# Splitting weights by one copy and one subtraction of 1024 columns instead of two of 512

## The chip, the cores and the metric

The kernel runs on one core of one Trainium2 chip. The metric is the device time of one execution in microseconds (us). Three executions of the kernel before took 1092.47, 1092.65 and 1095.68 us; their median is 1092.65 us.

## What is computed

The reference is a trunk of two layers over 256 tokens of width 1024, all in float32:

```
for l in range(2):
    x = x + 0.5 * swiglu(rms_norm(x), w_gate, w_up, w_down)   # "f1", inner width 2816
    h = rms_norm(x)
    p = h @ w_in                                              # 1024 -> 3328 columns
    x = x + concat(rwkv7(p[:, :1792]), retnet(p[:, 1792:])) @ w_out
    x = x + 0.5 * swiglu(rms_norm(x), w_gate, w_up, w_down)   # "f2"
out = rms_norm(x)
```

The RWKV-7 part (8 heads of 64) is a recurrence with decays, computed by chunks of 64 tokens: products within a chunk, the inverse of a triangle, and a state handed from chunk to chunk. The retention part has 4 heads.

## The kernel before

**Precision.** A plain float32 product is not used for the large matrices. Each operand is split into a rounded part `hi` and the rest `lo`, both of type float32r, and a product is three matmuls into one accumulator: hi by hi (line 189), hi by lo (line 190), lo by hi (line 191), all in `mm3`. For the activations this split is made once per token tile; for the weights it is made on the fly, by ScalarE and VectorE.

**Weights.** All weights lie in DRAM as 2 x 83 pieces of 128 x 2048, and are used as halves of 128 x 1024 (512 KB), 332 halves in all. `half(i, h)` loads half `h` of piece `i` into one of three raw buffers (`NRAW = 3`, SyncE's queue, line 169), and then, for each of its two 512-column chunks, copies the chunk to `whi` on ScalarE (line 176) and subtracts on VectorE, `wlo = raw - whi` (line 177). A raw buffer is free for the next load when the last subtraction from it is done. The tiles `whi` and `wlo` are 512 columns wide, in rings; there are four kinds of rings, by the stage that uses the piece: kind 0 for both feed-forwards (pieces 0 to 32 and 50 to 82 of a layer), kind 1 for the first two pieces of the mixer's projections, kind 2 for the other eleven, kind 3 for the four of the output projection. `NHL = (5, 4, 5, 6)` gives the halves that each ring holds, so 10, 8, 10 and 12 tiles of 512.

**Order of the work.** Tokens are two tiles of 128, `t = 0` and `t = 1`. Each is a Python generator that walks through all stages and yields after about one half of weights; `run` takes turns between them, with `t = 1` two steps behind (`LAG = 2`). So a half of weights is loaded and split once, used by `t = 0` in 6 matmuls, and some steps later by `t = 1` in 6 more; only then are its tiles free. Between the mixer and the second feed-forward the distance is larger: tile 0 begins the feed-forward (line 278 and following) while tile 1 still has the end of its mixer before it (`PLAN`).

The program is written without semaphores. A planner in the compiler (`auto_bufs=True`) plays the program through with modelled times, fixes by them the order of each engine's instructions, gives each tile an address in SBUF by the time that it lives, and puts in the waits. So the order on an engine is fixed when the kernel is built; at run time each engine takes its instructions in that order, and an instruction that has to wait holds up those behind it on its engine.

**Other lines that matter here.** `norm_T` transposes x (line 253) and makes its two parts, `parts` (lines 257 and 258). Line 239 is ScalarE's Square over 1024 columns with a sum. Lines 290 and 291 are the gate of the feed-forward, `to_features` transposes its result (line 272) and splits it (lines 213 and 214). `layer_vecs` loads a layer's small vectors on ScalarE's queue and makes two small tables on VectorE (lines 159 and 160). In the mixer, lines 346 to 499 and 575 to 581 are VectorE's work between the projections; line 783 multiplies retention scores that line 778 has masked.

The descriptor scratch is not named in the kernel before, so it has the default size.

Of the kernel before, what the change touches and what calls it, by code (L numbers as in the profile page):

```python
# [10 lines left out]
F32 = mybir.dt.float32  # L11
F32R = mybir.dt.float32r
BF16 = mybir.dt.bfloat16
AF = mybir.ActivationFunctionType
ALU = mybir.AluOpType
# [5 lines left out]
P = 128  # L21
# [12 lines left out]
HOT = 5  # L34
DEFER = (0, 16, 0)
MV = (0, 0, 0, 0, 0, 1)
NHL = (5, 4, 5, 6)
FIRST = 2
LAG = 2
PLAN = ("mkrqegRvJabcW...w", "mkrqegRvJabcW.....w")  # L40
PAUSE = (0, 2)
# [27 lines left out]


class Tiles:
    """Tiles of SBUF under names of their own, of which any number may be alive."""

    def __init__(self, pool):
        self.pool, self.n = pool, 0
# [14 lines left out]
class Trunk:  # L90
# [50 lines left out]
            self.nc.sync.dma_start(self.x[t][:, w * n:w * n + w], self.x_d[t][:, w * n:w * n + w])  # L141

    def few(self, n, name, bufs=1):
        """A few columns of a tile that all small things share, reused in turn."""
        if name not in self.rings:
            self.rings[name] = [0, self.nsmall]
            self.nsmall += n * bufs
            assert self.nsmall <= NBASE
        ring = self.rings[name]
        c = ring[1] + n * (ring[0] % bufs)  # L150
        ring[0] += 1
        return self.c[:, c:c + n]
# [8 lines left out]
        self.layer = l  # L161

    def half(self, i, h):
        """Half a piece of weights, split into two parts of 12 bits each."""
        if (i, h) not in self.wq:
            nc = self.nc
            raw = self.raw[:, self.nraw % NRAW]
            self.nraw += 1
            nc.sync.dma_start(raw, self.w_d[i][:, 1024 * h:1024 * h + 1024])
            kind = sum(i % PIECES >= b for b in (33, 33 + FIRST, 46, 50)) % 4  # L170
            parts = []
            for c in range(2):
                hi = self.A.get([P, 512], f"whi{kind}", F32R, 2 * NHL[kind])
                lo = self.A.get([P, 512], f"wlo{kind}", F32R, 2 * NHL[kind])
                src = raw[:, 512 * c:512 * c + 512]
                nc.scalar.activation(hi, src, AF.Copy)  # L176
                nc.vector.tensor_tensor(lo, src, hi.bitcast(F32), op=ALU.subtract)  # L177
                parts.append((hi, lo))
            self.wq[i, h] = parts
        return self.wq[i, h]  # L180

# [11 lines left out]
            self.catch_up(t, 1)  # L193

    def defer(self, t, count, f):
        """Emits f after some more products of the projections, and its own behind those."""
        if count:
            self.later[t].append([count, f])
        else:
            f()  # L200

    def catch_up(self, t, n=99):
        """Emits what has been deferred long enough."""
        for d in self.later[t]:
            d[0] -= n
        while self.later[t] and self.later[t][0][0] <= 0:
            f = self.later[t].pop(0)[1]
            with self.tc.issue_after(self.recent.ins):
                f()
# [10 lines left out]
            self.nc.vector.tensor_copy(out, x)  # L220

    def rsqrt(self, y, nx):
        """y = (-2 nx)^-1/2: a guess from the exponent, and Newton's steps."""
        nc = self.nc
        I32 = mybir.dt.int32
        TT, STT = nc.vector.tensor_tensor, nc.vector.scalar_tensor_tensor
        w = self.few(y.shape[1], "newton", 2)
        nc.vector.tensor_scalar(y.bitcast(I32), nx.bitcast(I32), 1, 0x3fffffff, op0=ALU.logical_shift_right, op1=ALU.bitwise_xor)
        nc.vector.tensor_scalar(y, y, GUESS, None, op0=ALU.mult)
        for _ in range(3):  # L230
            TT(w, y, y, op=ALU.mult)
            TT(w, w, nx, op=ALU.mult)
            STT(y, w, 1.5, y, op0=ALU.add, op1=ALU.mult)
# [25 lines left out]
                                               op0=ALU.mult, op1=ALU.subtract)  # L259
        self.rms(t, col)  # L260

# [1 line left out]
    def ffn(self, t, col, base, pause=()):  # L263
        nc = self.nc
        self.norm_T(t, col)
# [47 lines left out]
                                           op0=ALU.mult, op1=ALU.add)  # L313
        yield

# [1 line left out]
    def proj_block(self, t, base, blk):  # L317
        h0 = 0 if blk == 0 else 1 + 2 * (blk - 1)
        width = 256 if blk == 0 else 512
# [33 lines left out]
        return bc(self.v[:, off:off + 4], [P, 4, n])  # L353

    def half_sigmoid(self, out, ps, col):
        """sigmoid(ps + bias) as 0.5 + 0.5 tanh of half the argument."""
        nc = self.nc
        for p in range(NPAIR):
            nc.scalar.activation(out[:, p, :], ps[:, p, :], AF.Tanh, scale=0.5, bias=self.hv[:, col + p:col + p + 1])
        nc.vector.tensor_scalar(out, out, 0.5, 0.5, op0=ALU.mult, op1=ALU.add)  # L360

    def rwkv_decay(self, t, ps):
        """Decay, learning rate and gate, and the products of the decays from the start of a chunk."""
        nc, A, z = self.nc, self.A, self.z[t]
        TT, ACT, STT = nc.vector.tensor_tensor, nc.scalar.activation, nc.vector.scalar_tensor_tensor
        full = [P, 4, P]
        e, o = slice(0, 64), slice(64, 128)
        m0 = self.shifted(t, ps, 2, 0, 0)
        ACT(m0[0:64, 0, :], m0[0:64, 0, :], AF.Tanh)
        ACT(m0[:, 1, :], m0[:, 1, :], AF.Tanh, scale=0.5)  # L370
        nc.vector.tensor_scalar(m0[:, 1, :], m0[:, 1, :], 0.5, 0.5, op0=ALU.mult, op1=ALU.add)
        zw = self.ppr.tile(full, F32, name="pre")
        za = self.ppr.tile(full, F32, name="pre")
        zg = self.ppr.tile(full, F32, name="pre")
        lw, lg = self.lora
        for p in range(NPAIR):
            nc.tensor.matmul(zw[:, p, :], lhsT=lw[0:64, p * P:(p + 1) * P], rhs=m0[0:64, 0, :], start=True, stop=True)
        for p in range(NPAIR):
            nc.tensor.matmul(za[:, p, :], lhsT=lw[64:128, p * P:(p + 1) * P], rhs=m0[64:128, 0, :], start=True, stop=True)
        for p in range(NPAIR):  # L380
            nc.tensor.matmul(zg[:, p, :], lhsT=lg[:, p * P:(p + 1) * P], rhs=m0[:, 1, :], start=True, stop=True)
        sw = A.get(full, "sw")
        self.half_sigmoid(sw, zw, 14)
        a = A.get(full, "a")
        self.half_sigmoid(a, za, 18)
        g = A.get(full, "g")
        ACT(g, zg, AF.Copy)
        cs = A.get([P, 512], "cs")
        nc.vector.tensor_tensor_scan(cs, self.scan, sw.rearrange("p a b -> p (a b)"), 0.0,
                                     op0=ALU.mult, op1=ALU.add)  # L390
        pr = A.get([P, 8, CH], "pr")
        csv = cs.rearrange("p (a b) -> p a b", a=8)
        ACT(pr, csv, AF.Exp, scale=-KAPPA)
        ip = A.get([P, 8, CH], "ip")
        ACT(ip, csv, AF.Exp, scale=KAPPA)
        pc = self.few(16, f"pc{t}")[0:64].rearrange("q (a j h) -> q a j h", j=2, h=2)
        for h, q in enumerate((e, o)):
            ACT(pc[:, :, :, h], pr[q, :, CH - 1].rearrange("q (a j) -> q a j", j=2), AF.Copy)
        z.update(a=a, g=g, pr=pr, ip=ip, pc=pc)

    def rwkv_key(self, t, ps):
        """Keys, removal keys and their scaled forms."""
        nc, A, z = self.nc, self.A, self.z[t]
        TT, ACT, STT = nc.vector.tensor_tensor, nc.scalar.activation, nc.vector.scalar_tensor_tensor
        full = [P, 4, P]
# [1 line left out]
        a, pr, ip = z["a"], z["pr"], z["ip"]  # L407
# [52 lines left out]
        z.update(kh=kh, bk=bk, ar=ar, prv=prv, ck=ck)  # L460

    def rwkv_receptance(self, t, ps):
        """All products within a chunk, and the inverse of its triangle begun."""
        nc, A, z = self.nc, self.A, self.z[t]
        TT, ACT, STT = nc.vector.tensor_tensor, nc.scalar.activation, nc.vector.scalar_tensor_tensor
        full = [P, 4, P]
# [9 lines left out]
        dg = misc[:, 0:128].rearrange("q (j p i) -> q j p i", j=2, p=NPAIR)  # L476
# [65 lines left out]
        z.update(uvs=uvs, v=v)  # L542

    def inverse(self, t, dg, misc):
        """(I - L)^-1, transposed, of 8 heads in 2 chunks: dg holds the 16 x 16 diagonal blocks of L transposed,
        els all of it, one head above the other."""
        nc, A = self.nc, self.A
        TT, ACT = nc.vector.tensor_tensor, nc.scalar.activation
        full = [P, 4, P]
# [35 lines left out]
        return xc  # L585

    def merge(self, t):
        """From the inverses of the 16 x 16 diagonal blocks to those of the heads."""
        nc, A, n = self.nc, self.A, 16
        el, xc = self.z[t]["el"], self.z[t]["xc"]  # L590
        TT, ACT = nc.vector.tensor_tensor, nc.scalar.activation
# [2 lines left out]
        nc.gpsimd.memset(tt, 0.0)  # L594

        def products(rows, cols, at, lhs, rhs, width):
            """Products of blocks, those of a head and chunk next to each other in the array."""
            ps = self.ppr.tile([P, 2, NPAIR, width], F32, name="pre")
            for j in range(2):
                for p in range(NPAIR):  # L600
                    for q, c, r in zip(rows, cols, at):
                        nc.tensor.matmul(ps[r, j, p, :], lhsT=lhs[q, j, p, c], rhs=rhs[q, j, p, 0:width],
                                         start=True, stop=True)
            return ps
# [30 lines left out]
        self.z[t]["tts"] = [tt[:, j] for j in range(2)]  # L635

    def chain(self, t, j):
        """Chunk j of the token tile: the state before it and its own tokens, and the state after it."""
        nc, A, z = self.nc, self.A, self.z[t]
        assert self.nchunk == 2 * t + j  # L640
        self.nchunk += 1
# [356 lines left out]
def launch(arrays, stages):  # L998
    import concourse.bacc as bacc
    from concourse.bass_utils import run_bass_kernel_spmd  # L1000

    nc = bacc.Bacc("TRN2", target_bir_lowering=False, num_devices=1)
    feeds, args = {}, []
    for name, v in arrays.items():
        v = np.ascontiguousarray(v)
# [6 lines left out]
```

## Time and profile before

| | us |
|---|---|
| median of three runs | 1092.65 |
| lowest, highest | 1092.47, 1095.68 |
| span of the profiled execution | 1094.5 |
| TensorE (PE) busy | 1067.3 |
| VectorE (DVE) busy | 712.8 |
| ScalarE (ACT) busy | 626.5 |
| mean granted clock of TensorE | 0.995 |
| weight loads, issue to landing (median) | 4.3 |

The profile gives one execution, whose own time is its span. An engine's busy time is the time in which at least one of its instructions runs; ends of matmuls are modelled and overlap the next one, so a busy PE is not a PE at its peak. "Idle before" is the time for which an engine stood still just before the instructions of a group, and "<-" names what ended it.

### The profile page before, as it was taken

To read this page: it belongs to the slowest core of one execution; us is meant where nothing else is said; L and a number is where in the kernel's file an instruction comes from. 1 tells how busy PE (TensorE), PEld (TensorE's weight loads), DVE (VectorE), ACT (ScalarE), POOL (GpSimd) and SP (SyncE) were. 2 spreads that over 40 slices of the span, in tenths; PEclk is the share of its full clock that TensorE was granted. 3 is DMA by queue.
4 is the path that set the end of the run, shared out by engine and by line. 5 is a ranking of instruction groups with operands and counts; after the bars stand their busy time and mean duration, and the time that the engine had idled before them with its cause. 6 is when DMAs were issued, how large, how long until landed. Compare 5 with 4: busy or idle time off the path is not lost.

```text
span 1094.5 us, 16902 instructions
## 1 busy us (share of the span) xinstructions
PE 1067.3 (98%) x6253; PEld 862.0 (79%) x6253; DVE 712.8 (65%) x1527; ACT 626.5 (57%) x1344; POOL 17.8 (2%) x36
## 2 busy tenths in 40 slices
PE   7999999999999999999999999999999999999997
PEld 5888878878777788888888888878777778888886
DVE  5655556778988565555575556557899776655564
ACT  6554545775777464545364445548677856545453
POOL 1000000000000000000000000000000000000000
PEclk8999999999999999999999999999999999999999
DMA  7755555523533165555555565553343344565652
GB/s 255 240 192 191 194 184 184 172 81 132 145 115 130 59 211 193 186 196 196 173 172 191 175 197 189 185 198 117 117 139 96 114 136 135 192 191 183 201 175 78
DMA packets 59298, 180.84 MB, mean 165 GB/s; under 512 B 14288, under 2 KB 14928, under 8 KB 59216
## 3 DMA queue, kind: packets, MB, share of 16 engines
q1 hardware_dynamic: 58784, 179.63, 50.6%
q8 instruction: 49, 0.80, 0.3%
q14 instruction: 33, 0.27, 0.1%
q10 hardware_dynamic: 432, 0.13, 0.1%
HBM read 178.17 MB, written 1.57 MB: 164 GB/s over the span
## 4 chain that ended last, share of the span: by engine, by line
PE 74%; DVE 9%; DMA 8%; ACT 7%; issue 1%; SPq 0%; POOLq 0%; POOL 0%; ACTq 0%
PE gu L191 17%; PE gu L189 17%; PE gu L190 17%; DMA base<-in_w 7%; PE pre L190 3%; PE pre L191 3%; PE pre L189 3%; DVE wlo L177 3%; PE ch L190 3%; PE ch L189 3%; PE ch L191 3%; PE tr L272 2%; ACT whi L176 1%; DVE prod L575 1%; DVE lw L485 1%
## 5 line engine op out<-in xcount | busy, mean ns | idle before, releaser
L177 DVE TENSOR_TENSOR wlo<-base,whi 128x512 fp32r<-128x512 f32 x664 | 433.0, 687 | 149.8 <-ACT whi L176 107.1
L176 ACT ACTIVATE whi<-base 128x512 fp32r<-128x512 f32 x664 | 386.1, 624 | 172.9 <-DMA base<-in_w 125.2
L189 PE MATMUL gu<-whi,parts 128*128 128x512 f32 (+1 forms) x928 | 366.6, 398 | 6.6 <-ACT parts L257 3.5
L190 PE MATMUL gu<-wlo,parts 128*128 128x512 f32 (+1 forms) x928 | 360.8, 390 | 2.7 <-DVE wlo L177 2.7
L191 PE MATMUL gu<-whi,parts 128*128 128x512 f32 (+1 forms) x928 | 361.3, 390 | 0.2 <-DVE parts L258 0.2
L189 PEld LDWEIGHTS gu<-whi,parts 128*128 128x128 f32 x928 | 174.9, 189 | 46.1 <-ACT parts L257 8.8
L190 PEld LDWEIGHTS gu<-wlo,parts 128*128 128x128 f32 x928 | 175.3, 189 | 37.3 <-DVE wlo L177 5.4
L191 PEld LDWEIGHTS gu<-whi,parts 128*128 128x128 f32 x928 | 174.9, 189 | 37.3 <-DVE parts L258 2.0
L290 ACT ACTIVATE hh<-gu,base 128x256 f32<-128x256 f32 x88 | 41.6, 474 | 144.9 <-PE gu L191 144.7
L291 DVE SCALAR_TENSOR_TENSOR hh<-gu,base,hh 128x256 f32<-128x256 f32 x88 | 42.5, 483 | 105.6 <-ACT hh L290 105.6
L191 PE MATMUL ch<-whi,ht 128*128 128x512 f32 x176 | 70.4, 400 | 0.0
L191 PE MATMUL pre<-whi,ht 128*128 128x512 f32 x176 | 70.3, 400 | 0.0
L189 PE MATMUL ch<-whi,ht 128*128 128x512 f32 x176 | 69.0, 392 | 0.0
L190 PE MATMUL ch<-wlo,ht 128*128 128x512 f32 x176 | 68.8, 391 | 0.0
L190 PE MATMUL pre<-wlo,ht 128*128 128x512 f32 x176 | 68.8, 391 | 0.0
L189 PE MATMUL pre<-whi,ht 128*128 128x512 f32 x176 | 68.6, 390 | 0.0
L213 ACT ACTIVATE ht<-tr 128x256 fp32r<-128x256 f32 x88 | 33.1, 376 | 55.1 <-PE tr L272 35.0
L214 DVE TENSOR_TENSOR ht<-tr,ht 128x256 fp32r<-128x256 f32 x88 | 37.0, 420 | 41.0 <-ACT ht L213 41.0
L190 PEld LDWEIGHTS pre<-wlo,ht 128*128 128x128 f32 x176 | 33.0, 188 | 7.1
L190 PEld LDWEIGHTS ch<-wlo,ht 128*128 128x128 f32 x176 | 33.1, 188 | 6.7
L189 PEld LDWEIGHTS pre<-whi,ht 128*128 128x128 f32 x176 | 33.1, 188 | 6.2
L191 PEld LDWEIGHTS pre<-whi,ht 128*128 128x128 f32 x176 | 33.1, 188 | 6.2
(202 smaller groups left out, 972.3 us busy)
## 6 DMA issues: line engine op xcount, KB each, us to landing
base<-in_w SPq DMA_DIRECT2D x332, 512.0 KB, 4.3
lora<-in_lora SPq DMA_DIRECT2D x4, 256.0 KB, 5.9
out<-ot SPq DMA_DIRECT2D x4, 256.0 KB, 2.2
base<-in_consts SPq DMA_DIRECT2D x1, 805.0 KB, 8.5
base<-in_x SPq DMA_DIRECT2D x2, 256.0 KB, 3.2
base<-in_x SPq DMA_DIRECT2D x1, 512.0 KB, 8.7
fg<-in_fgain SPq DMA_DIRECT2D x2, 256.0 KB, 6.2
d<-misc SPq DMA_DIRECT2D x4, 64.0 KB, 4.4
```

The lines of the kernel that those rows point to most:

```text
L176: nc.scalar.activation(hi, src, AF.Copy)
L177: nc.vector.tensor_tensor(lo, src, hi.bitcast(F32), op=ALU.subtract)
L189: nc.tensor.matmul(ps, lhsT=ah, rhs=wh, start=start, stop=False)
L190: nc.tensor.matmul(ps, lhsT=ah, rhs=wl, start=False, stop=False)
L191: self.recent = nc.tensor.matmul(ps, lhsT=al, rhs=wh, start=False, stop=stop)
L213: nc.scalar.activation(hi, src, AF.Copy)
L214: nc.vector.tensor_tensor(lo, src, hi.bitcast(F32), op=ALU.subtract)
L272: nc.tensor.transpose(tr[:, j, :], hh[:, j * P:(j + 1) * P], self.ident)
L290: nc.scalar.activation(hh, ps[:, 0:256], AF.Silu, scale=R)
L291: nc.vector.scalar_tensor_tensor(hh, ps[:, 256:512], R, hh, op0=ALU.mult, op1=ALU.mult)
L485: TT(lw, gp, mask, op=ALU.mult)
L575: TT(p3, left.unsqueeze(2).to_broadcast(sh), right.rearrange("u k j -> u j k").unsqueeze(1).to_broadcast(sh), op=ALU.mult)
```

## The change

`half` makes one tile `whi` and one tile `wlo` of 1024 columns for a half, and fills each by one instruction: one copy on ScalarE, one subtraction on VectorE. The first four halves (`2 * i + h < NARROW`) still fill them by two instructions of 512 columns each. The rings now count tiles of 1024 columns; those of kinds 2 and 3 hold 4 and 5 halves instead of 5 and 6, those of kinds 0 and 1 hold as much as before. The matmuls read the same 512 columns at a time as before, as slices of the wide tiles. The descriptor scratch is set to 1024 bytes for each partition. Some docstrings and comments are dropped.

```diff
-NHL = (5, 4, 5, 6)
+NHL = (5, 4, 4, 5)
 FIRST = 2
+NARROW = 4
...
             kind = sum(i % PIECES >= b for b in (33, 33 + FIRST, 46, 50)) % 4
-            parts = []
-            for c in range(2):
-                hi = self.A.get([P, 512], f"whi{kind}", F32R, 2 * NHL[kind])
-                lo = self.A.get([P, 512], f"wlo{kind}", F32R, 2 * NHL[kind])
-                src = raw[:, 512 * c:512 * c + 512]
-                nc.scalar.activation(hi, src, AF.Copy)
-                nc.vector.tensor_tensor(lo, src, hi.bitcast(F32), op=ALU.subtract)
-                parts.append((hi, lo))
+            hi = self.A.get([P, 1024], f"whi{kind}", F32R, NHL[kind])
+            lo = self.A.get([P, 1024], f"wlo{kind}", F32R, NHL[kind])
+            width = 512 if 2 * i + h < NARROW else 1024
+            for c in range(0, 1024, width):
+                s = slice(c, c + width)
+                nc.scalar.activation(hi[:, s], raw[:, s], AF.Copy)
+                nc.vector.tensor_tensor(lo[:, s], raw[:, s], hi[:, s].bitcast(F32), op=ALU.subtract)
+            parts = [(hi[:, c:c + 512], lo[:, c:c + 512]) for c in (0, 512)]
             self.wq[i, h] = parts
...
-    nc = bacc.Bacc("TRN2", target_bir_lowering=False, num_devices=1)
+    nc = bacc.Bacc("TRN2", target_bir_lowering=False, num_devices=1, dynamic_dma_scratch_size=1024)
```

## Rows read from the trace of the kernel before

**Rows 1.** The page's first part: busy us (share of the span) xinstructions.

```profile
PE 1067.3 (98%) x6253; PEld 862.0 (79%) x6253; DVE 712.8 (65%) x1527; ACT 626.5 (57%) x1344; POOL 17.8 (2%) x36
```

**Rows 2.** Windows: stretch, its length, busy us of PE, PEld, DVE, ACT, POOL; clock, DMA.

```profile
40.00:200.00 160.00, 160.00 (x727) 131.13 (x726) 92.66 (x160) 80.36 (x160) 0.55 (x1) 1.00 0.59 196
...
200.00:240.00 40.00, 38.46 (x227) 31.90 (x227) 28.77 (x76) 31.79 (x83) 0.93 (x1) 1.00 0.35 119
240.00:320.00 80.00, 76.44 (x621) 60.44 (x620) 72.79 (x207) 54.86 (x128) 3.20 (x6) 1.00 0.41 119
...
380.00:720.00 340.00, 337.71 (x1534) 277.91 (x1535) 197.89 (x354) 172.65 (x349) 1.10 (x2) 1.00 0.57 187
...
780.00:860.00 80.00, 77.36 (x645) 61.00 (x645) 73.64 (x208) 56.09 (x130) 2.83 (x4) 1.00 0.40 120
```

**Rows 3.** Timeline of PE from 100 us: start us, us, engine line op tiles.

```profile
100.01 0.39 PE L191 MATMUL gu<-whi,parts 128*128 128x512 f32 x1
100.24 0.39 PE L189 MATMUL gu<-whi,parts 128*128 128x512 f32 x1
```

**Rows 4.** Waits of PE over the whole span: total us, times, longest us.

```profile
PE tr L783 <- DVE sc L778: 3.9, 4, 1.0
PE gu L189 <- ACT parts L257: 3.5, 5, 1.6
PE gu L189 <- ACT whi L176: 2.8, 1, 2.8
PE gu L190 <- DVE wlo L177: 2.7, 3, 2.3
```

**Rows 5.** Groups by line: xcount | busy us, mean ns | idle before, what ended it.

```profile
L177 DVE TENSOR_TENSOR wlo<-base,whi 128x512 fp32r<-128x512 f32 x664 | 433.0, 687 | 149.8 <-ACT whi L176 107.1 <-issue 14.6 <-PE gu L190 10.0
L176 ACT ACTIVATE whi<-base 128x512 fp32r<-128x512 f32 x664 | 386.1, 624 | 172.9 <-DMA base<-in_w 125.2 <-PE ch L191 20.7 <-PE gu L191 18.7
...
L239 ACT ACTIVATE junk<-base 128x1024 bf16<-128x1024 f32 x12 | 12.7, 1057 | 8.7 <-DVE base L312 6.6 <-DMA base<-in_x 1.5 <-DVE base L859 0.6
...
L454 DVE TENSOR_TENSOR bk<-kh,ip 128x256 f32<-128x256 f32 x8 | 3.3, 417 | 0.0
```

**Rows 6.** Timelines of ACT and DVE from 388 us: one half split, pairs merged.

```profile
389.36 1.16 ACT L176 ACTIVATE whi<-base 128x512 fp32r<-128x512 f32 x2 [2.15 <-DMA base<-in_w]
...
390.03 1.29 DVE L177 TENSOR_TENSOR wlo<-base,whi 128x512 fp32r<-128x512 f32 x2 [1.94 <-ACT whi L176]
```

**Rows 7.** Windows of line 177 alone, in the middle of both mixers.

```profile
240.00:320.00 80.00, 22.33 (x34) 1.00 0.41 119
780.00:860.00 80.00, 24.37 (x37) 1.00 0.40 120
```

**Rows 8.** The chain that ended last, from 244 us: start us, us, what.

```profile
244.20 0.61 DVE wlo L177
244.86 4.64 DMA base<-in_w
249.52 0.64 ACT whi L176
250.18 0.69 DVE wlo L177
```

**Rows 9.** Waits of PEld and PE in 240 to 320 us, by line group.

```profile
L189 PEld LDWEIGHTS gu<-whi,parts 128*128 128x128 f32 x66 | 12.4, 188 | 3.0 <-ACT whi L176 0.5
L190 PEld LDWEIGHTS gu<-wlo,parts 128*128 128x128 f32 x65 | 12.2, 188 | 3.0 <-DVE wlo L177 0.9
```

**Rows 10.** Timelines of PE, ACT and DVE from 371 us, the second feed-forward's start.

```profile
371.17 0.39 PE L191 MATMUL gu<-whi,parts 128*128 128x512 f32 x1
...
371.23 0.62 ACT L176 ACTIVATE whi<-base 128x512 fp32r<-128x512 f32 x1
...
371.89 0.69 DVE L177 TENSOR_TENSOR wlo<-base,whi 128x512 fp32r<-128x512 f32 x1 [0.17 <-ACT whi L176]
...
372.78 0.63 PE L190 MATMUL gu<-wlo,parts 128*128 128x512 f32 x2
```

**Rows 11.** Timelines of DVE and PE from 376 us, the longest of PE's waits for wlo.

```profile
376.49 0.69 DVE L177 TENSOR_TENSOR wlo<-base,whi 128x512 fp32r<-128x512 f32 x1 [0.48 <-ACT whi L176]
380.76 0.17 DVE L159 TENSOR_SCALAR base<-base 128x14 f32<-128x14 f32 x1 [3.58 <-DMA base<-in_vecs]
...
381.51 1.29 DVE L177 TENSOR_TENSOR wlo<-base,whi 128x512 fp32r<-128x512 f32 x2
...
382.26 0.50 PE L190 MATMUL gu<-wlo,parts 128*128 128x512 f32 x1 [2.26 <-DVE wlo L177]
```

**Rows 12.** The page's third part: DMA queue, kind: packets, MB, share of 16 engines.

```profile
q1 hardware_dynamic: 58784, 179.63, 50.6%
...
q10 hardware_dynamic: 432, 0.13, 0.1%
```

## The prediction

> **What bounds the kernel now.** I read the busy times first. TensorE (PE) is busy for 1067.3 of 1094.5 us, VectorE (DVE) for 712.8, ScalarE (ACT) for 626.5 [rows 1]: the end is set by PE, and this change touches no matmul. Then the windows, to see where PE is not full [rows 2]. In the feed-forwards it has no gap at all (160.00 of 160.00 us), with DVE and ACT at 58% and 50%. In the middle of each mixer PE lacks 3.56 us of 80 (240 to 320) and 2.64 us of 80 (780 to 860), and there DVE is 91% and 92% busy. So DVE paces the mixers' middle in part, and nothing else in the kernel. The timeline gives PE's real pace, one matmul of 512 columns every 0.227 us [rows 3]; a half of weights feeds 12 of them, 2.72 us. Last, what PE waits for [rows 4]: weights cost it 2.8 us once at the very start (where the change keeps the narrow split) and 2.7 us in three places later, of which one is 2.3. All that faster splitting could give back at once is a few us; the rest would have to come through DVE in the mixers.
>
> The profiled execution spans 1094.5 us, 1.85 more than the median of 1092.65. Terms are read from the one and applied to the other.
>
> **Price of a wide split.** A subtraction of 512 columns takes 0.687 us and one VectorE operation of 256 columns 0.417 [rows 5], so 512 further columns cost 512/256 x 0.270 = 0.54, and the wide one takes about 1.23 us (an estimate; no row shows one). Two narrow ones back to back take 1.29 [rows 6]: saved 0.06 us of DVE for a half. If they stand apart, 2 x 0.687 - 1.23 = 0.15. A copy of 1024 columns: ACT has one operation of that width, 1.057 us (line 239) [rows 5]; two narrow copies take 1.16 back to back [rows 6], so 0.10 is saved, or 2 x 0.624 - 1.057 = 0.19 apart. Over 328 halves that is 20 to 49 us of DVE and 33 to 62 us of ACT, nearly all in the feed-forwards beside a full PE, worth nothing there.
>
> The Trainium skill (VectorE: DVE Perf Modes, section "The TRN2 errata") states that a float32 tensor_tensor pays about 150 cycles at 0.96 GHz per instruction whatever its width; by it a half would save 0.157 us, 51 us in all. The trace's 0.06 for the usual back-to-back pair disagrees: the second instruction hides most of that fixed part. By the page the next term would be -5.6 instead of -2.1.
>
> **DVE in the mixers.** 34 and 37 subtractions fall into the two crowded stretches [rows 7], 17 and 18.5 halves. At 0.06 that frees 1.0 + 1.1 = 2.1 us; at 0.15, 2.6 + 2.8 = 5.4, below PE's gaps of 6.2 there [rows 2]. At the other end, 0: PE's recorded waits there are for single results (line 778's scores, [rows 4]) and need not end earlier. I take -2.1, since both pairs in rows 6 stand back to back.
>
> **ACT.** Between 200 and 240 us ACT is busy 31.8 of 40 [rows 2], and `parts` from ACT hold PE up for 3.5 us in all [rows 4]. Some 4 halves for each layer fall there: 8 x 0.10 = 0.8, at most 8 x 0.19 = 1.5, at least 0. I take -0.6.
>
> **Later first chunk.** Now a copy starts at 389.36, the first `wlo` is done at 390.03 + 0.69 = 390.72, the second at 391.32 [rows 6]. Wide: 1.06 + 0.05 + 1.23 = 2.34 after the start. The first chunk is 0.98 us later, the second, and with it the raw buffer, 0.38. In the feed-forwards this is covered: a ring of five halves is 5 x 2.72 = 13.6 us of PE work, of which two or three are in use by the two token tiles, so a split is ready about two halves, 5 us, ahead (an estimate), and 0.98 fits. Without that cover each half would cost up to 0.98. In the mixers' middle weights are just in time: the chain runs from a subtraction over a load (4.64) to a copy and a subtraction again [rows 8], and the weight loads of PE wait 0.5 and 0.9 us for line 176 and line 177 in one layer's stretch [rows 9]. That is some two events; if each were 0.98 later in both layers, 2 x 2 x 0.98 = 3.9; at least 0, as other matmuls may be put in front. I take +0.8, nearer to PE's own wait on `wlo`, which is small there.
>
> **Second feed-forward's start.** Token tile 0 runs ahead until the ring is full of halves that tile 1 has not used. A chunk is then freed by tile 1's matmul at 371.17, copied at 371.23, subtracted at 371.89 to 372.58 and used at 372.78 [rows 10]: no slack. With wide tiles the slot is free only after the second chunk's three matmuls too (3 x 0.227 = 0.68), and the split takes 0.98 longer: 1.66 us. PE has tile 1's five halves to run meanwhile, if the planner puts them there. For two layers between 0 and 3.3; I take +1.0.
>
> **The blocked subtraction.** At 376.49 DVE subtracts one chunk of a half; line 159 comes next in its order, stands 3.58 us for the small vectors' load, and the second chunk is only done after it, so PE idles 2.26 [rows 11]. A wide subtraction is one instruction, before or behind line 159. Before it, the stall goes (-2.3); behind it, both chunks come late, by 0.54 more for the work and the first chunk's lead of 0.69 lost: +1.2. What comes next in line, the following half, is needed 3 us later. I take -1.1.
>
> **Smaller rings.** Kind 2 holds one half less before the crowded stretch. That half's split (1.23 us) then moves into it, for at most 2 x 1.23 = 2.5, at least 0 because a raw buffer still holds the half. I take +0.5. Kind 3's weights are used in the mixer's calm end; 0 there. What hides this is DVE's idle 7 us of 80 [rows 2]; if that is elsewhere, the upper end holds.
>
> **Scratch.** All transfers of data run in queues marked hardware_dynamic [rows 12], so no cost is seen for a smaller scratch; more room can only spare waits on reused addresses, of which PE shows none by name: 0.
>
> Sum: -2.1 - 0.6 + 0.8 + 1.0 - 1.1 + 0.5 = -1.4 us, from 1092.65 to **1091.2**. Ends added up: -5.4 - 1.5 - 2.3 = -9.2, and 3.9 + 3.3 + 1.2 + 2.5 = +10.9.
>
> **Rivals.**
> 1. *DVE gives back the mixers.* For it: DVE at 91% there, and pairs that other work separates save 0.15. Against: PE's gaps there are only 6.2 us. All of -5.4, the stall of rows 11 gone (-2.3), ACT -0.6, and the costs as above except the stall's (+2.3): -6.0, 1086.6 us.
> 2. *Weights come late* (the other side). In the places without slack the wide split makes the first chunk wait for the second's copy: rows 9 and 10 priced in full, 3.9 + 3.3 = 7.2, rings 1.0, less 2.7 for DVE and ACT: +5.5, 1098.2 us. It decides once PE's waits on lines 176 and 177, 5.5 us now [rows 4], exceed about 11. Against it: the planner knows the longer durations and can put other matmuls first. The Trainium skill (Perfetto Trace Analysis, "Optimizing Scalar/DVE Operations") puts the case: where these engines aren't saturated but cause bubbles elsewhere, breaking instructions up may let work finish sooner, and this change does the reverse; where they are saturated, larger operations help. Both places exist here, the first in rows 10, the second in rows 2.
> 3. *It doesn't do what it says*: a wide instruction costs what two did (1.29, 1.16), or the planner's new order undoes it; then latency alone is left, about +1, 1093.7.
>
> **Chances.** About 0.3% (3.3 us) is what a measurement of this kernel can tell from no change. Forecast 0.38, its own range 1089.4 to 1095; rival 1 0.34; rival 2 0.23; rival 3 0.05. Faster 0.36 (rival 1 and a little of the forecast's edge), same 0.39, slower 0.25 (rival 2 and some of rival 3). A new order of all engines can move any term, so the 8-in-10 range reaches most of the way to both sums of ends: 1084.5 to 1099.5.
>
> **What would show it.** 332 copies and subtractions and four more of each, about 1.06 and 1.23 us long; DVE busy 660 to 695, ACT 565 to 595. PE full from 40 to 200 us as now. The wait at line 159 without, or with, a PE stall on `wlo` behind it. PE's gaps in the two crowded stretches: near 4 together for the forecast, near 0 for rival 1. PE's waits on lines 176 and 177: under 6, or over 11 for rival 2. The forecast is wrong if the feed-forwards show gaps, or if the mixers' length changes by over 3 us.

## The result and the profile after

The changed kernel takes 1123.95 us (median of 4, 1118.97 to 1127.87) against 1093.6 for the kernel before in the same comparison: 1.0279 times as long [1.0257, 1.0302], 30 us slower. That lies outside the predicted range of 1084.5 to 1099.5 and on the other side. The profiled execution spans 1126.0 us. In the kernel after, all lines from 39 on stand one further down: the copy is line 177, the subtraction 178, the three products 190 to 192.

The page's first part and two of its strips (40 equal slices; PE's digits are tenths of busy time, PEclk's tenths of TensorE's full clock), to be held against [rows 1]:

```profile
PE 1086.1 (96%) x6253; PEld 876.6 (78%) x6253; DVE 691.6 (61%) x1199; ACT 604.1 (54%) x1016; POOL 18.2 (2%) x36
...
PE   7999999999898999999999999999999979999997
...
PEclk8999999999976999999999999999999979999999
```

The splitting engines have less to do, DVE by 21 us and ACT by 22. But PE is busy 18.8 us longer with the same 6253 matmuls, and its clock is lower in two places, at the ends of the two mixers (slices 12 and 13, and 33). The mean granted clock is 0.974 where it was 0.995: (1 - 0.974) x 1126.0 = 29.3 us of clock not granted, against 0.005 x 1094.5 = 5.5.

The groups of the wide split, which answer to [rows 5]:

```profile
L178 DVE TENSOR_TENSOR wlo<-base,whi 128x1024 fp32r<-128x1024 f32 x328 | 400.8, 1223 | 293.3 <-ACT whi L177 292.0 <-ACT sv L655 0.4 <-issue 0.3
L177 ACT ACTIVATE whi<-base 128x1024 fp32r<-128x1024 f32 x328 | 346.6, 1059 | 323.3 <-PE gu L192 130.2 <-PE ch L192 111.8 <-DMA base<-in_w 55.0
```

Windows of the kernel after, columns as in [rows 2]. 240 to 320 and 780 to 860 are the crowded stretches of the prediction, 240 to 280 and 800 to 840 parts of them; the others are the ends of the mixers:

```profile
240.00:320.00 80.00, 76.61 (x568) 60.88 (x569) 71.92 (x186) 52.55 (x106) 2.89 (x6) 1.00 0.42 129
780.00:860.00 80.00, 76.97 (x428) 62.16 (x427) 68.77 (x164) 54.37 (x104) 0.42 (x2) 1.00 0.39 122
240.00:280.00 40.00, 40.00 (x214) 32.92 (x214) 35.90 (x74) 24.25 (x43) 0.43 (x2) 1.00 0.51 167
...
322.00:343.00 21.00, 20.84 (x338) 17.72 (x339) 10.02 (x22) 12.32 (x29) 0.00 (x0) 0.51 0.19 54
343.00:353.00 10.00, 7.38 (x88) 5.14 (x86) 7.82 (x20) 7.06 (x12) 0.00 (x0) 1.00 0.30 101
353.00:367.00 14.00, 11.62 (x109) 9.21 (x109) 8.96 (x11) 6.77 (x12) 0.52 (x1) 0.51 0.65 204
...
800.00:840.00 40.00, 40.00 (x210) 32.94 (x209) 34.26 (x73) 25.50 (x46) 0.00 (x0) 1.00 0.49 156
...
900.00:920.00 20.00, 13.35 (x157) 10.41 (x157) 11.51 (x16) 8.72 (x15) 0.00 (x0) 0.66 0.62 198
```

Two of them in the kernel before:

```profile
322.00:343.00 21.00, 20.54 (x395) 15.76 (x389) 16.97 (x43) 17.07 (x39) 0.00 (x0) 1.00 0.33 108
353.00:367.00 14.00, 13.57 (x63) 10.18 (x62) 9.26 (x30) 5.04 (x13) 0.56 (x1) 1.00 0.15 46
```

The gaps that DVE was to give back have moved, but not shrunk. Parts of the crowded stretches are now entirely full (240 to 280, 800 to 840), yet over the whole of both PE lacks 3.39 + 3.03 = 6.4 us, where it lacked 6.2. (Layer 1's mixer begins 17.6 us later here; counted from its beginning, the same 80 us lack 3.4.) In each of them PE now waits 1.1 us or more for a wide copy and 1.3 for a wide subtraction, where it waited 0.2 for a subtraction before.

The large price stands behind them. Of 21 us from 322, TensorE was granted 0.51, its lower level of 1.2 GHz, while its record says busy 20.84; again from 353, and in the second layer. The not granted part of these three stretches is 21 x 0.49 + 14 x 0.49 + 20 x 0.34 = 24 us; it is not lost one for one, as the groups below show. PE's recorded idle time in the two mixers (the stages named below) grows as well, from 12.0 to 27.3 us.

What runs there, in PE's timeline of the kernel after:

```profile
317.40 0.40 PE L192 MATMUL gu<-whi,parts 128*128 128x512 f32 x1
...
319.25 0.40 PE L190 MATMUL gu<-whi,rh 128*128 128x512 f32 x1
...
321.93 0.24 PE L603 MATMUL pre<-tc,x 32*32 32x32 f32 x2 [0.97 <-ACT x L219]
...
323.28 1.12 PE L666 MATMUL ch<-sv,lw 128*64 128x64 f32 x16
...
325.16 1.12 PE L671 MATMUL ch<-wt,tt 64*64 64x64 f32 x16
...
332.01 0.80 PE L190 MATMUL gu<-whi,rh 128*128 128x512 f32 x1
...
340.54 0.80 PE L191 MATMUL gu<-wlo,rh 128*128 128x512 f32 x1
...
353.47 1.08 PE L721 MATMUL ch<-base,yn 128*128 128x128 f32 x4 [3.08 <-DVE yn L718]
```

And the same steps in the kernel before (lines 665 and 670 there are 666 and 671 here):

```profile
317.74 0.69 PE L665 MATMUL ch<-sv,lw 128*64 128x64 f32 x16
318.35 0.50 PE L191 MATMUL gu<-whi,rl 128*128 128x512 f32 x1
318.69 0.39 PE L189 MATMUL gu<-whi,parts 128*128 128x512 f32 x1
319.26 0.68 PE L670 MATMUL ch<-wt,tt 64*64 64x64 f32 x16
319.87 0.50 PE L191 MATMUL gu<-whi,parts 128*128 128x512 f32 x1
```

The end of a mixer is a row of dependent steps, the state handed from chunk to chunk (`chain`, lines 666 to 721 here), each a group of small matmuls of 64 columns. Before, large matmuls of the projections or of a later product stand between most of the groups. After, the last projection (`gu<-whi,parts`) runs at 317.40, 6 us ahead of the first chain product, and from 319.25 the next large matmul is 12.8 us away (332.01). At the third chain it is 12.0 us (349.99 to 362.00), with a wait of 3.08 us for `yn` in it. From the start of layer 0's first chain to that of its third, before has 39 large matmuls in 23.2 us, 6 of them of the projections; after has 29 in 31.2 us, none of them of the projections. In these groups 16 matmuls take 1.12 us where they took 0.69, a large one 0.80 where it took 0.39 to 0.50. In layer 1 the counts are the same, 39 and 29, but at its first two chains the clock was low for some 3 us only (878.8 to 882.2), and the stretch went from 23.5 us to 24.8. So the missing large matmuls alone do not fix the price.

### The profile page after: what moved, and what is told of

Read it like the earlier page. It is cut to its first block, busy times and chain, and to the rows that moved or that the text cites. A ratio compares the mean times of both kernels' runs of the same rounds, so it can differ in the third digit from the quotient of the medians.

```text
span 1126.0 us, 16242 instructions
## 1 busy us (share of the span) xinstructions
PE 1086.1 (96%) x6253; PEld 876.6 (78%) x6253; DVE 691.6 (61%) x1199; ACT 604.1 (54%) x1016; POOL 18.2 (2%) x36
## 4 chain that ended last, share of the span: by engine, by line
PE 77%; DVE 8%; ACT 8%; DMA 6%; issue 1%; SPq 0%; POOLq 0%; POOL 0%; ACTq 0%
PE gu L190 17%; PE gu L192 17%; PE gu L191 17%; DMA base<-in_w 5%; PE pre L190 3%; PE pre L191 3%; PE pre L192 3%; PE ch L191 3%; PE ch L192 3%; PE ch L190 3%; DVE wlo L178 3%; ACT whi L177 2%; PE tr L273 2%; DVE prod L576 1%; PE pre L603 1%
## 5 line engine op out<-in xcount | busy, mean ns | idle before, releaser
L178 DVE TENSOR_TENSOR wlo<-base,whi 128x1024 fp32r<-128x1024 f32 (+1 forms) x336 | 406.1, 1211 | 295.5 <-ACT whi L177 294.1
L177 ACT ACTIVATE whi<-base 128x1024 fp32r<-128x1024 f32 (+1 forms) x336 | 351.5, 1049 | 325.1 <-PE gu L192 130.2
L190 PE MATMUL gu<-whi,parts 128*128 128x512 f32 x928 | 364.1, 396 | 11.0 <-ACT whi L177 6.6
L192 PE MATMUL gu<-whi,parts 128*128 128x512 f32 x928 | 359.6, 390 | 0.6 <-DVE parts L259 0.3
L191 PE MATMUL pre<-wlo,ht 128*128 128x512 f32 x176 | 72.4, 411 | 0.0
L258 ACT ACTIVATE parts<-tr,base 128x128 fp32r<-128x128 f32 x96 | 31.5, 362 | 18.3 <-PE tr L254 9.1
L190 PEld LDWEIGHTS pre<-whi,ht 128*128 128x128 f32 x176 | 33.0, 188 | 7.0
L192 PEld LDWEIGHTS ch<-whi,ht 128*128 128x128 f32 x176 | 33.0, 188 | 6.9
L190 PEld LDWEIGHTS ch<-whi,ht 128*128 128x128 f32 x176 | 33.0, 188 | 6.8
L259 DVE SCALAR_TENSOR_TENSOR parts<-tr,base,parts 128x128 fp32r<-128x128 f32 x96 | 30.6, 346 | 11.9 <-ACT parts L258 10.4
```

Of the source, the lines that this page charges most:

```text
L177: nc.scalar.activation(hi[:, s], raw[:, s], AF.Copy)
L178: nc.vector.tensor_tensor(lo[:, s], raw[:, s], hi[:, s].bitcast(F32), op=ALU.subtract)
L190: nc.tensor.matmul(ps, lhsT=ah, rhs=wh, start=start, stop=False)
L191: nc.tensor.matmul(ps, lhsT=ah, rhs=wl, start=False, stop=False)
L192: self.recent = nc.tensor.matmul(ps, lhsT=al, rhs=wh, start=False, stop=stop)
L258: nc.scalar.activation(xh[:, k], ps[:, j], AF.Copy, scale=gain)
```

## The experiments

Ratios are to the kernel before, measured beside each kernel on the same chip, with 95% intervals. The stage "mixer 0" is the time from the first feed-forward's last gate to the next one's first (by ScalarE's instructions of line 290), 225.6 us before and 246.0 after; "mixer 1" is the same stage of layer 1, 226.0 and 239.3. Part of token tile 1's mixer lies behind the end of a stage.

**One part alone.** Only the smaller rings, in the kernel before:

```diff
-NHL = (5, 4, 5, 6)
+NHL = (5, 4, 4, 5)
```

> Kernel before with its 512-column tiles and two splits for a half, but the rings of kinds 2 and 3 one half smaller (8 and 10 tiles of 512). Theory A (the clock: with wide splits in the mixer the planner uses up the large matmuls early, a stretch of small matmuls alone follows, and TensorE's granted clock falls to its lower level there): rings alone don't do it, 1090 to 1097 us, mean clock 0.99 or more. Theory B (smaller rings starve the mixer): 1112 us or more, clock under 0.985. Theory C (a wide split is late where weights are just in time): 1090 to 1097 us, like A.

Measured: 1103.88, 1.0099 [1.0073, 1.0125]; mixer 0 232.5 us, mixer 1 230.5. The smaller rings alone cost 10.7 us.

The changed kernel with every half split by narrow instructions, into wide tiles:

```diff
-NARROW = 4
+NARROW = 9999
```

> Changed kernel, but every half is split by two copies and two subtractions of 512 columns, so only the tiles are wide (freed by halves), the rings smaller and the scratch smaller. Theory A: no long wide instruction, so the planner keeps the large matmuls among the small ones: 1090 to 1098 us, clock 0.99 or more. Theory B, or coarser freeing as the cause: 1112 us or more. Theory C: 1090 to 1098 us.

Measured: 1109.81, 1.0148 [1.0116, 1.018]; 5.9 us over the smaller rings alone, with the intervals just overlapping.

Wide tiles and splits in the feed-forwards alone, the rings as before. It has the small scratch, and so have the next one and all that build on it:

```diff
+            if kind == 0:
+                hi = self.A.get([P, 1024], f"whi{kind}", F32R, NHL[kind])
...
+            else:
+                for c in range(2):
```

> Wide tiles and wide splits for the feed-forwards alone (kind 0); the mixer's three kinds as in the kernel before, with its ring sizes; scratch 1024. Theory A: mixers keep their order, 1088 to 1096 us, clock 0.99 or more. Theory B: the same. Theory C: also near the kernel before, but the start of the second feed-forward loses 1 to 4 us: 1094 to 1098 us.

Measured: 1092.29, 0.9983 [0.9968, 0.9998], a gain of 0.9 us by the medians, not to be told from none by our bound of 0.3%.

The reverse, `if kind > 0` with the smaller rings:

> The other way round: wide tiles, wide splits and the smaller rings for the mixer's kinds 1, 2 and 3; the feed-forwards as in the kernel before; scratch 1024. Theory A: all of the loss is here, 1115 to 1130 us, mean clock 0.97 to 0.98, lower level in the last third of both mixers. Theory B: the same. Theory C: loss of 5 to 12 us by waits on copies and subtractions, clock 0.99: 1098 to 1106 us.

Measured: 1129.86, 1.0332 [1.0289, 1.0375], granted clock 0.971. The whole loss sits with the mixers' weights, their wide splits and smaller rings together; the feed-forwards' wide splits do no harm. The strip of the clock has the same two places (slices 12 and 13, 32 and 33):

```profile
PEclk9999999999987999999999999999999679999999
```

**Is it the clock, and does it come from the wide splits in the mixer?** Two theories stood: the loss is waits for late weights (rival 2), or it is TensorE's clock in a stretch with too few large matmuls. The first kernel keeps all splits wide and adds work: two products of constants (128 x 128 by 256 columns, bfloat16), which the real ones then overwrite, ahead of each group of chain products, and likewise ahead of the 32-wide groups in `merge`.

```diff
+FILL = 2
+    def fill(self, ps):
...
+        for _ in range(FILL):
+            self.nc.tensor.matmul(flat, lhsT=self.scan[:, :P], rhs=self.scan[:, :256], start=True, stop=True)
...
+        self.fill(wa)
...
+        self.fill(u)
```

> Changed kernel with 2 extra matmuls of 256 bf16 columns (constants, overwritten by the real products) before each group of small matmuls in chain() and in the 32-wide groups of merge(): 31 groups for a layer's mixer, some 124 matmuls of about 0.11 us in all, 14 us of PE if nothing hides them. Theory A (a large part of the loss is TensorE's clock, which falls to its lower level while only small matmuls run): the clock stays at its upper level in both mixers, clock loss under 5 us instead of 26, and the time falls in spite of the added work: 1105 to 1117 us. Rival D (the loss is in the chain of dependent small steps on ScalarE and VectorE, the clock only shows it): the fillers change nothing or add their own time: 1123 to 1138 us.

Measured: 1104.81, 1.0095 [1.0076, 1.0114]: 84 matmuls that compute nothing make the changed kernel 19 us faster. Its window and timeline at the same place (line 593 is the filling):

```profile
320.00:343.00 23.00, 22.68 (x443) 17.04 (x437) 16.86 (x41) 17.33 (x38) 0.00 (x0) 1.00 0.21 71
```

```profile
323.88 0.39 PE L593 MATMUL ch<-base 128*128 128x256 bf16 x2
324.20 0.69 PE L700 MATMUL ch<-sv,lw 128*64 128x64 f32 x16
324.82 0.68 PE L702 MATMUL ch<-uv,lq 64*64 64x64 f32 x16
...
343.32 0.50 PE L193 MATMUL gu<-whi,rl 128*128 128x512 f32 x1
```

The clock stays at 1.00, the groups are back at 0.69, and mixer 0 falls from 246.0 to 232.2. The plan is made anew for this kernel too. At the first two chains that is no return of the old order: the longest distance between two of the kernel's own large matmuls is still 11.1 us, and from the first chain to the third there are 27, none of the projections. There the filling is the main difference, and the clock stays whole; the pause of 0.97 us ahead of the fall is gone too. At the third chain it is not the filling alone: large matmuls stand between the groups again (343.32 is one), and the waits for `yn` and `uv` are gone. PE's idle time in the two mixers is 13.3 us instead of 27.3. How much of the 19 us is the clock's, and how much the idle time's, this run does not separate.

The second leaves the splits wide in the feed-forwards and makes them narrow in the mixers, with the tiles and rings of the changed kernel:

```diff
-            width = 512 if 2 * i + h < NARROW else 1024
+            width = 512 if 2 * i + h < NARROW or kind else 1024
```

> Changed kernel, with the mixer's halves (kinds 1, 2, 3) split by two narrow instructions in their wide tiles; feed-forwards split wide; smaller rings, smaller scratch. If the wide instructions in the mixer are what lowers the clock: 1104 to 1112 us, like the run with all splits narrow (1109.8), clock 0.99. If the wide tiles and rings do it in the planner's order: 1119 us or more.

Measured: 1104.08, 1.0085 [1.0067, 1.0104]; the clock is whole and the longest distance between large matmuls in the mixers 6.8 us (5.9 in the kernel before):

```profile
320.00:343.00 23.00, 22.75 (x418) 17.63 (x419) 17.79 (x44) 19.06 (x43) 0.00 (x0) 1.00 0.26 82
```

So the wide splits of the mixers' weights cost 1123.95 - 1104.08 = 19.9 us (by the two ratios, 21). That they do it by way of the order is read from the traces: the clock is whole again here and PE's idle time in the mixers 18.9 us. What is left in both kernels, some 10 us over the kernel before, is about what the smaller rings cost alone; that it is the same loss is not shown.

**Kind 2 by itself.** Wide splits for kind 2 only (`if kind == 2`), its ring at five halves:

> Kernel before with wide tiles and wide splits for kind 2 alone (eleven projection pieces of a mixer), its ring at 5 halves as before; all else as before, scratch 1024. If the smaller rings are needed for the loss: 1090 to 1098 us. If wide splits in the projections suffice to use up the large matmuls early: 1105 us or more and a clock under 0.985. Coarser freeing alone (6 us between the runs with smaller rings and narrow or wide tiles): about 1099 us.

Measured: 1102.11, 1.0074 [1.005, 1.0098], granted clock 0.987 to 0.992. The wide splits cost 8 us in kind 2 even with the whole ring. With the ring at four and narrow splits, in the kernel before (`NHL = (5, 4, 4, 6)`):

> Kernel before with only kind 2's ring one half smaller (8 tiles of 512), kind 3's as before. If kind 2's ring carries the 10.7 us of the run with both smaller: 1101 to 1106 us. If kind 3's does: 1090 to 1096 us. If both share it: 1097 to 1100 us.

Measured: 1103.17, 1.0073 [1.0048, 1.0097], 8.7 us: most of what both smaller rings cost, kind 2's alone costs. Where, the trace of the kernel with both smaller rings shows. First windows of PE (length, busy, granted clock, DMA) and DVE's line 562 in the kernel before:

```profile
260.00:280.00 20.00, 19.62 (x119) 1.00 0.39 113
280.00:300.00 20.00, 18.98 (x116) 1.00 0.45 124
...
340.00:360.00 20.00, 19.45 (x204) 1.00 0.55 181
```

```profile
280.60 0.16 DVE L562 COPY mx<-mx 64x8 f32<-64x8 f32 x1
```

Then the same windows with both smaller rings, and the timelines of DVE and of PE:

```profile
260.00:280.00 20.00, 16.53 (x105) 1.00 0.47 139
280.00:300.00 20.00, 19.93 (x117) 0.91 0.35 93
...
340.00:360.00 20.00, 16.58 (x188) 1.00 0.59 186
```

```profile
273.07 0.34 DVE L346 SCALAR_TENSOR_TENSOR shd<-tr,base,shd 128x127 f32<-128x127 f32 x1
276.40 0.17 DVE L562 COPY mx<-mx 64x8 f32<-64x8 f32 x1 [2.99 <-DMA mx<-d]
...
276.56 0.41 DVE L471 TENSOR_TENSOR ar<-shd,pr 128x256 f32<-128x256 f32 x1
```

```profile
278.61 1.68 PE L483 MATMUL tr<-ar,bk 64*128 64x128 f32 x16 [3.25 <-DVE ar L471]
```

Counted from the first feed-forward's last gate (141.5 us before, 137.7 here), DVE comes to line 562, which needs a small table's way through DRAM, 3.4 us earlier than before and stands 2.99 us for that transfer; `ar`, for the next products, is queued behind it, PE waits 3.25 us, and then its clock dips as well. From 340 to 360 PE has gaps where it had few: from the first chain on only 2 large matmuls of the projections are left, where there were 6. Over the whole of mixer 0, which is 6.9 us longer, PE's idle time grows from 6.1 to 9.9 us, and 0.09 x 20 = 1.8 us of clock are not granted. This is read from the trace; no run took that wait away alone, and for mixer 1 the place stays open.

**The scratch.** The kernel before with `dynamic_dma_scratch_size=1024`:

> Kernel before with the smaller descriptor scratch alone. Every theory: 1091 to 1096 us, no difference.

Measured: 1093.64, 0.9995 [0.9974, 1.0016]. Every engine runs the same order as before. It costs nothing. (Wide tiles with the old rings throughout, and the changed kernel with the default scratch, were not run.)

**A better version.** The feed-forwards wide, and the room used the other way, for a longer ring of kind 2, `NHL = (5, 4, 6, 6)`:

> Wide splits for the feed-forwards alone, and kind 2's ring one half larger than before (6 halves) in the room that the smaller scratch leaves. If what the smaller ring cost (8 to 11 us) is a steady price of reach ahead, one half more gives some of it back the other way: 1083 to 1090 us. If five halves were enough: 1090 to 1094 us, as with wide feed-forwards alone (1092.3).

Measured: 1090.24, 0.9964 [0.9947, 0.9981]: better than both kernels, by 3.9 us over the kernel before. Its interval overlaps that of the wide feed-forwards alone, so how much is the sixth half's isn't separated.

A fourth raw buffer instead (`NRAW = 4`, `NHL = (5, 4, 5, 6)`), and both together:

> Wide splits for the feed-forwards alone, and four raw buffers instead of three, so loads may start one half earlier. If copies that wait for a load (125 us of ScalarE's idle time before) hold up the mixers: 1083 to 1090 us. If that idle time costs nothing: 1089 to 1094 us.

> Both: wide splits for the feed-forwards alone, kind 2's ring at 6 halves, four raw buffers. If the two help by the same reach ahead, about the better of them: 1082 to 1090 us; if neither does: 1089 to 1094 us.

Measured: 1093.04, 0.9992 [0.9976, 1.0009], and 1092.14, 0.9992 [0.9975, 1.001]. More room for loads buys nothing that these runs can tell, and with it the sixth half's gain does not show.

## Why the prediction was wrong

**"DVE in the mixers" (-2.1, ends -5.4 and 0) is the step that failed.** It took DVE's freed time for PE's: faster splits were to close part of the 6.2 us of gaps in the two crowded stretches. DVE's time was freed at the price foreseen, but the gaps are 6.4 us now; rival 1, which had them near 0, holds for parts of the stretches alone. The step held PE's order fixed and asked only how long each wait would be, while the sentence on the planner ("a new order of all engines can move any term") was used to widen the range by a few us. Not priced was the other side of a new order: large matmuls that run earlier are missing later, at the mixer's end, where before they stood between the dependent small steps. There the mixers grew, by 20.5 and 13.3 us, where the prediction called itself wrong from 3 us on. With fillers 19 of 30 us are back; with narrow splits in the mixers, 20.

The upper end of that step, 0, was therefore no bound. The granted clock was read as a mean of 0.995 and never as a thing that the change could lower. "Later first chunk" (+0.8, end 3.9) was small as well: PE's waits for wide copies and subtractions in the two crowded stretches are 2 x (1.1 + 1.3) = 4.8 us, where 0.4 stood before. Rival 3 had a new order that undoes the gain, but left only +1 for it. The sum has a slip that changes nothing: its terms add up to -1.5, not -1.4, and 1091.2 stands.

**"Smaller rings" (+0.5, ends 0 and 2.5) is the second, a term mis-sized by a factor of 20**: both rings cost 10.7 us alone, kind 2's 8.7 (1103.17 - 1094.51). I priced the half's split as work that moves into the crowded stretch. What the trace shows is another order of DVE and PE: DVE stands at a transfer (2.99 us) that was covered before, and PE runs short of projections at the mixer's end.

**Rival 2** foresaw the side, not the cause. Its deciding sign was PE's waits on the two split lines over 11 us; they are 9.2, of which 3.4 stand at the start. The rows of the kernel after have other waits beside them:

```profile
PE gu L190 <- ACT whi L177: 6.6, 5, 3.4
PE ch L721 <- DVE yn L718: 6.2, 2, 3.1
PE ch L677 <- ACT uv L672: 4.1, 2, 2.7
PE gu L190 <- ACT parts L258: 4.1, 5, 1.4
PE gu L191 <- DVE wlo L178: 2.6, 2, 1.3
```

Two of them are new but for 0.4 us, `yn` and `uv`, 10.3 us together, at the chain itself. For `uv`, ACT's timeline shows what is queued ahead, and for `yn`, DVE's:

```profile
357.27 1.06 ACT L177 ACTIVATE whi<-base 128x1024 fp32r<-128x1024 f32 x1 [1.23 <-DMA base<-in_w]
358.23 0.36 ACT L672 ACTIVATE uv<-ch 64x256 f32<-64x256 f32 x1
```

```profile
351.03 0.16 DVE L232 TENSOR_TENSOR base<-base 128x8 f32<-128x8 f32 x1
351.10 1.22 DVE L178 TENSOR_TENSOR wlo<-base,whi 128x1024 fp32r<-128x1024 f32 x1
352.24 0.16 DVE L233 TENSOR_TENSOR base<-base 128x8 f32<-128x8 f32 x1
...
352.63 0.69 DVE L718 TENSOR_TENSOR yn<-y,base 128x512 f32<-128x512 f32 x1
```

A wide copy that waits for its load holds ScalarE for 2.3 us, and a small result of the chain stands behind it. A wide subtraction of 1.22 us stands between two small steps that lead to `yn`, within PE's wait of 3.08. That is the "later first chunk" turned round: not the matmul of the weights is late, but what queues behind the copy.

**What was right.** The prices: 1.223 us for the subtraction (1.23 predicted), 1.059 for the copy (1.06), 336 of each, DVE busy 691.6 (660 to 695). ACT's 604.1 lies over its 565 to 595: a half saved 22.4 / 328 = 0.07 us there, not 0.10 to 0.19. PE is full from 40 to 200 us (159.85 of 160), so the feed-forwards hid all of it. The stall behind the small vectors' table is gone: two wide subtractions now run ahead of it (396.67 to 399.2 us), line 160 then waits for nothing, and from the second feed-forward's first gate to token tile 0's last it went from 118.2 to 116.0 us. That fits the -2.3 of that term with nothing left for "second feed-forward's start" (+1.0); no run separates the two. ACT's -0.6 did not come: `parts` hold PE up for 4.1 us instead of 3.5. The scratch is 0.

## What to carry to other kernels

When a fixed order is planned anew, relief at one place is work taken from another: look where the engine's large matmuls are filling time between dependent small ones, and count them there before and after, as one counts waits. A ring's depth is reach for the planner, not only room for data: one half of weights in 5 was worth some 8 us, while the 43.6 us of DVE's and ACT's work that the change saved (21.2 + 22.4) gave nothing that these runs can tell. And the mean granted clock went from 0.995 to 0.974 with the same 6253 matmuls in another order; it belongs among the terms of a sum.

## What the hardware showed unexpectedly

TensorE's granted clock stood at its lower level while the engine was recorded busy without a pause, 20.40 of the 20.40 us from 322.5. Before it fell, PE had left the large matmuls at 319.6 us and run small ones, with recorded pauses of 0.97 and 0.16 us; the level rose again at 342.9, behind five large ones in a row from 340.54. The Trainium skill (TensorE: Matmul & The Clock Gate, section "HAM oscillation — how this bites in real kernels") tells of such falls where the engine waits for data between batches. The other two long falls agree with that: at 353.2 and 902.7 us the level went down as PE's waits of 3.08 us for `yn` were ending. For the first, pauses are here too (0.97 us ahead of the fall), but for all of the time at the lower level the record has none. Small matmuls alone do not hold the level down either. In layer 1 the same steps, with pauses of 0.96 and 0.16 us ahead, lowered it at 878.8, and it was back while small ones still ran:

```profile
879.00:882.00 3.00, 3.00 (x47) 2.49 (x45) 1.32 (x3) 2.42 (x7) 0.00 (x0) 0.50 0.15 27
882.30:891.00 8.70, 8.56 (x267) 7.30 (x265) 4.97 (x12) 5.75 (x17) 0.00 (x0) 1.00 0.32 111
```

With 84 small fillers in both mixers the level stayed at 1.00, though that kernel has a pause of 1.10 us at 315.4. That the mixture of matmuls matters is likely from that run; which property of them does, and why the two layers differ, no run separates.
